# Steps of a triangular inverse offered to two engines, and a TensorE order that stays in a part of the array, in a hybrid gMLP and RWKV-7 block

## The chip, the cores and the metric

One core of a Trainium2 chip runs the whole block in one launch. The metric is the device time of one execution in microseconds (us); the median of three executions is compared. TensorE (PE) multiplies, VectorE (DVE) and ScalarE (ACT) and GpSimd (POOL) work element by element, and the queue of SyncE (SP) issues every DMA.

## The reference

Input and output are 1024 tokens by 1024 channels in float32. What the kernel must compute, cut to what matters here:

```python
def reference(x, ...):
    h = rms_norm(x, norm_pre_g)
    p = h @ w_in                                  # 9344 columns
    ya = gmlp_branch(p[gmlp columns], ...)        # u * (W_s LN(v) + b) * silu(z)
    yb = rwkv7_branch(p[rwkv columns], ...)       # the recurrence below, 16 heads of 64
    merged = sigmoid(ga) * (ya @ w_branch_a) + sigmoid(gb) * (yb @ w_branch_b)
    return x + rms_norm(merged @ w_out, norm_post_g)

def step(state, inp):                             # RWKV-7, for each token of each head
    r_t, w_t, k_t, v_t, kk_t, a_t = inp
    sa = einsum('bhvk,bhk->bhv', state, -kk_t)
    state = state * w_t + outer(sa, kk_t * a_t) + outer(v_t, k_t)
    o_t = einsum('bhvk,bhk->bhv', state, r_t)
```

## The kernel before

The channels lie on the partitions. The large products run as three float32r matmuls of split operands (high by high, high by low, low by high), each 128x128 weights by 512 columns; these are the **dense** matmuls (`ps<-hm,whi`, `ps<-hm,wlo`). The kernel has four stages: the norm and the gMLP branch, up to about 450 us; the RWKV branch, up to about 1240 us, into whose second half the product with `w_branch_a` is laid; the product with `w_branch_b` and the merge; the output product and norm.

The recurrence is computed in chunks of 64 tokens. The function `half_unit` does one **unit**, two heads by 512 tokens (eight chunks); there are 16 units, and every line of it is called once a unit. Its steps, with the names that the profile shows:

1. Preparation: decays, keys and queries are scaled into `W` and `BK`. Two groups of eight matmuls of 64-row weights (`pg<-W,BK`) give the chunk matrices; DVE masks them into `Pm` (the strictly triangular one), `BA` and `W`.
2. The triangular inverse. SP stores the 32x32 diagonal blocks of `Pm` to `bs_d` and loads them back as `X`, so that each of the 128 partitions holds one block; it loads `Q`, the identity. Then the 31 steps of the loop `for t in range(31, 0, -1)`, each a product `qt<-X,Q` and a sum `Q<-Q,qt`, one depending on the other: 62 instructions in a row, with 8 to 76 elements a partition (50 on average). SP stores `Q` to `ts_d` and loads it back as `N`; four DVE transposes write it into `Pm`.
3. Assembling the 64x64 inverse: groups of small matmuls on parts of the array, 32x64 (`pg<-N,Pm`, which is where TensorE first needs the inverse), 64x32, 64x64 and 64x128 (`pg<-BA,X`).
4. The chain over the chunks: `pc<-Z,W`, scaled on ACT and DVE into the next `Z`; then the outputs (`pg<-W,Z`, 128x64), the head norm (`sh`, `sl`, `bdr`), the gate, and a store to `yb_d`, which the third stage loads again.

The order of instructions on every engine is written by `Sched`, a list scheduler. The functions call its queues (`G` for POOL, `V` for DVE, `A` for EITHER); `call` records every instruction, its tiles and an estimated cost, and `flush` lays them out. At each turn it takes, over all engines, the ready instruction that could start first, and among those with an equal start the one of the smallest priority (`CHAIN` 0, `INV` 1, `PREP` 2.5, `LATE` 4, `DENSE` 9). An EITHER instruction is offered to DVE and to POOL; its start on POOL counts as 400 ns (`SLOWER`) later than it is. On TensorE an instruction whose weights need another size of the array than the one before starts `DRAIN` later. The cost rules are linear in the elements: for a two-input instruction `(62 + n) / .96` ns on DVE, and `2.1 * n + 152` on POOL. What the scheduler thinks fixes the order alone; on the chip each engine runs its list from the top and waits where an operand is not there.

Of the kernel before, what the change touches and what calls it, by code (L numbers as in the profile page):

```python
# [14 lines left out]
ALU = mybir.AluOpType  # L15
# [3 lines left out]
P = 128  # L19
# [42 lines left out]
class Sched:  # L62
# [13 lines left out]
            "Sqrt": ("Sqrt",), "Ln": ("Ln",)}  # L76
    SWITCH = 1.5
    SLOWER = 400
    DRAIN = 150

    def __init__(self, nc, tc=None, plan=None):
        self.nc, self.tc, self.plan = nc, tc, plan
# [157 lines left out]
    def flush(self):  # L240
        if self.plan is not None:
            for i in self.plan.orders[self.nflush]:
                self.tc.keep_in_program_order(self.calls[i]())
                self.calls[i] = None
            self.nflush += 1
            return
        ops, b0, n = self.ops, self.done, len(self.ops)
        self.ends += [0.0] * (n - b0)
        self.start += [0.0] * (n - b0)
        ends = self.ends  # L250
        left, succ, users = {}, {}, {}
        for i in range(b0, n):
            d = [j for j in ops[i][1] if j >= b0]
            left[i] = len(d)
            for j in d:
                succ.setdefault(j, []).append(i)
            for t in ops[i][2]:
                users[t] = users.get(t, 0) + 1
        state = self.__dict__.setdefault("state", {})
        where = self.__dict__.setdefault("where", {})  # L260
        lastend = self.__dict__.setdefault("lastend", {})
        self.slot += [None] * (self.ntile - len(self.slot))
        nxt = {}
        for t in range(self.ntile):
            if t not in where:
                nxt.setdefault(self.group[t], []).append(t)
        for g in nxt:
            nxt[g] = nxt[g][::-1]
        ready = {e: [] for e in self.free}

        def push(i):
            for eng in ("DVE", "POOL") if i in self.took else (ops[i][0],):
                t = 0.0
                for j in ops[i][1]:
                    t = max(t, ends[j] + self.LATENCY[ops[j][0]][self.ENGINES.index(eng)])
                ready[eng].append((t, i))

        bank = {}

        def when(t, i, eng):  # L280
            want = {}
            for v in ops[i][2]:
                if v in where:
                    t = max(t, where[v])
                    for e, x in bank.get(v, {}).items():
                        if e != eng:
                            t = max(t, x + 200)
                    continue
                g = self.group[v]
                want[g] = want.get(g, 0) + 1  # L290
                if self.bufs[g][1] and nxt[g][-1] != v:
                    return None
            for g, m in want.items():
                s = state.setdefault(g, [])
                for h in [h for h in self.heirs.get(g, ()) if not nxt.get(h)]:
                    self.heirs[g].remove(h)
                    self.places[g] += [(h, k) for k in range(len(state[h]))]
                    s += state[h]
                m -= max(0, self.bufs[g][0] - len(s))
                if m <= 0:  # L300
                    continue
                f = sorted(lastend[u] for u in s if not users.get(u))
                if len(f) < m:
                    return None
                t = max(t, f[m - 1])
            if ops[i][8]:
                t = max(t, self.port["POOL" if eng == "DVE" else "DVE"])
            return t

        for i in range(b0, n):  # L310
            if left[i] == 0:
                push(i)
        order = []
        while len(order) < n - b0:
            best = None
            for e, r in ready.items():
                for t, i in r:
                    t = when(t, i, e)
                    if t is None:
                        continue  # L320
                    t = max(t, self.free[e])
                    p = ops[i][4]
                    if self.switch(ops[i][5]):
                        p = (p[0] + self.SWITCH, p[1])
                    key = (t + (self.SLOWER if e == "POOL" and i in self.took else 0), p)
                    if best is None or key < best[0]:
                        best = key, e, i, t
            if best is None:
                raise RuntimeError("the schedule is stuck: " + str(
                    [(e, [(i, ops[i][7], [(v, self.group[v]) for v in ops[i][2] if v not in where]) for t, i in r][:6])  # L330
                     for e, r in ready.items()]))
            _, e, i, s = best
            for r in ("DVE", "POOL") if i in self.took else (e,):
                ready[r] = [x for x in ready[r] if x[1] != i]
            eng, deps, tiles, dur, prio, table, size, _, port = ops[i]
            if i in self.took:
                self.took[i] = eng = e
                if e == "POOL":
                    dur = size
                ops[i] = (eng, deps, tiles, dur, *ops[i][4:])  # L340
            for v in tiles:
                if v not in where:
                    g = self.group[v]
                    st = state[g]
                    if len(st) < self.bufs[g][0]:
                        self.slot[v], where[v] = len(st), 0.0
                        st.append(v)
                    else:
                        k = min((k for k in range(len(st)) if not users.get(st[k])), key=lambda k: lastend[st[k]])
                        self.slot[v], where[v] = k, lastend[st[k]]  # L350
                        st[k] = v
                    nxt[g].remove(v)
                    self.used.append(v)
            if eng == "SP":
                self.start[i] = s
                self.free[e] = s + dur
                self.hw = max(s + dur, self.hw) + size[1]
                self.dq = max(self.hw + 650, self.dq) + size[0] / 360.0
                ends[i] = self.dq + 950
            else:  # L360
                if self.switch(table):
                    s += 1290
                if eng == "PE" and size != self.array:
                    self.array, s = size, s + self.DRAIN
                if table:
                    self.table = table if self.table is None or self.switch(table) else self.table
                self.start[i] = s
                self.free[e] = ends[i] = s + dur
                if port:
                    self.port[e] = s + dur  # L370
            order.append(i)
            for v in tiles:
                users[v] -= 1
                if self.group[v][0] == "psum":
                    bank.setdefault(v, {})[eng] = ends[i]
                lastend[v] = max(lastend.get(v, 0.0), ends[i] + (eng != "SP") * 200)
            for k in succ.get(i, ()):
                left[k] -= 1
                if left[k] == 0:
                    push(k)  # L380
        self.orders.append(order)
        self.done = n
# [43 lines left out]
def half_unit(S, I, rw, dram, bank, p, h, r, k0, v, zz, uh, ul, bdr, xw, xa, Z, KI, vec, con, hv, eps, yb):  # L426

    mm, transpose, act, dma = S.PE.matmul, S.PE.transpose, S.ACT.activation, S.SP.dma_start
    V, G, A, at = S.DVE, S.POOL, S.EITHER, S.at
# [89 lines left out]
    for a in range(4):  # L519
        i = a % 2  # L520
        dma(bs_d[:, a].rearrange("c s t -> s c t"), Pm[32 * a:32 * a + 32, :, 32 * i:32 * i + 32])
    B = rw.tile([P, 32, 32], F32, name="X", bufs=2, fifo=False)
    for j in range(4):
        dma(B[32 * j:32 * j + 32].rearrange("p s t -> p (s t)"), bs_d.rearrange("c a s t -> (c a) (s t)"))
    Q = rw.tile([P, 8, 32], F32, name="Q", bufs=2)
    dma(Q.rearrange("p m s -> p (m s)"), I["q0"])
    qt = rw.tile([P, 8, 32], F32, name="qt", bufs=1)
    for t in range(31, 0, -1):
        m0 = t // 4
        G.tensor_tensor(qt[:, m0:, 0:t], B[:, 0:t, t].unsqueeze(1).broadcast_to([P, 8 - m0, t]),  # L530
                        Q[:, m0:, t].unsqueeze(2).broadcast_to([P, 8 - m0, t]), op=ALU.mult)
        G.tensor_tensor(Q[:, m0:, 0:t], Q[:, m0:, 0:t], qt[:, m0:, 0:t], op=ALU.add)
    ts_d = dram.tile([4, 8, 4, 8, 32], F32, name="ts_d", bufs=2)
    dma(ts_d.rearrange("q c a m s -> (q c a) (m s)"), Q.rearrange("p m s -> p (m s)"))
    N = rw.tile([P, 8, 32], F32, name="N", bufs=1)
# [2 lines left out]
    for a in range(4):  # L538
        i = a % 2
# [842 lines left out]
```

## Time and profile before

| | |
|---|---|
| median of 3 executions | 1429.69 us (1426.26 to 1430.96) |
| the profiled execution | 1426.28 us |
| its span, first to last instruction | 1424.1 us |
| busy: PE, DVE, ACT, POOL | 95%, 79%, 52%, 37% |
| mean granted clock of TensorE | 0.976 |
| steps of the inverse | 992 instructions, all on POOL |

A row of the timeline gives the start of an instruction from the span's first, how long it took, engine, line, operation, tiles written and read, shape and count; in square brackets stands the idle time of the engine in front of it and what ended it. All instructions are recorded through one line (L134), so they are told apart by their tiles.

### The profile page before, as it was taken

The page shows a single profiled execution, that of the slowest core. Times are in us where ns is not written, and L with a number is a line of the kernel's source. Part 1 is how long each engine was busy: PE and PEld are TensorE (multiplying, and loading weights), DVE is VectorE, ACT ScalarE, POOL GpSimd, SP SyncE. Part 2 cuts the span into 40 slices and gives each one's busy share as a digit, 9 for nine tenths or more (in the row PEclk, how much of TensorE's full clock was granted, in tenths as well). Part 3 has the DMA queues.
Part 4 walks back from the last instruction along what each step waited for, and adds up shares of the span by engine and source line. Part 5 has one row for each costly group of instructions (what it writes and reads, how often), then busy time and mean ns, then how long its engine had stood idle before and what let it go on. Part 6 is the DMA issues. An engine that isn't in the chain of part 4 may idle for free.

```text
span 1424.1 us, 23358 instructions
## 1 busy us (share of the span) xinstructions
PE 1347.4 (95%) x8390; PEld 1075.0 (75%) x8390; DVE 1118.8 (79%) x2034; ACT 742.6 (52%) x1340; POOL 525.8 (37%) x1135
## 2 busy tenths in 40 slices
PE   5899999999999999999998989999899899979997
PEld 3787888888878777777776767777677677858785
DVE  7977888887865868888788877888788575599957
ACT  6626444444444656667655567666666353433223
POOL 0002000001121176756566663776745553043211
PEclk9899999999999999999999999999999899989999
DMA  7102434447775211222211212211135756254456
GB/s 250 45 1 96 155 134 148 141 140 228 263 249 205 64 56 38 67 71 67 64 46 45 57 53 64 61 54 48 53 99 165 230 177 226 88 202 170 140 215 242
DMA packets 109523, 175.12 MB, mean 123 GB/s; under 512 B 43488, under 2 KB 53856, under 8 KB 109408
## 3 DMA queue, kind: packets, MB, share of 16 engines
q1 hardware_dynamic: 109408, 173.64, 36.8%
q8 instruction: 66, 1.08, 0.3%
q14 instruction: 49, 0.40, 0.1%
HBM read 121.17 MB, written 52.43 MB: 122 GB/s over the span
## 4 chain that ended last, share of the span: by engine, by line
PE 67%; DVE 13%; ACT 9%; DMA 6%; issue 4%; SPq 1%; POOL 1%; DVEq 0%; ACTq 0%; POOLq 0%
PE ps L134 37%; PE pg L134 25%; PE pc L134 5%; DVE hm L134 2%; DVE Pm L134 2%; ACT L134 2%; DVE W L134 1%; DMA hm<-ya_d 1%; DVE pg L134 1%; ACT Z L134 1%; DVE BK L134 1%; DVE wlo L134 1%; SPq L134 1%; ACT BA L134 1%; ACT KI L134 1%
## 5 line engine op out<-in xcount | busy, mean ns | idle before, releaser
L134 PE MATMUL ps<-hm,whi 128*128 128x512 f32 x1616 | 538.7, 405 | 5.3 <-DMA hm<-ya_d 4.7
L134 PEld LDWEIGHTS ps<-hm,whi 128*128 128x128 f32 x1616 | 301.8, 191 | 69.9 <-DMA hm<-ya_d 9.8
L134 PE MATMUL ps<-hm,wlo 128*128 128x512 f32 x808 | 326.8, 405 | 1.1 <-DVE wlo L134 1.1
L134 POOL TENSOR_TENSOR qt<-X,Q 128x60 f32<-128x60 f32 (+24 forms) x496 | 204.5, 412 | 91.3 <-DMA X<-bs_d 39.0
L134 POOL TENSOR_TENSOR Q<-Q,qt 128x60 f32<-128x60 f32 (+24 forms) x496 | 196.1, 395 | 37.9
L134 PEld LDWEIGHTS ps<-hm,wlo 128*128 128x128 f32 x808 | 154.1, 191 | 33.6 <-DVE wlo L134 3.1
L134 PE MATMUL pg<-pg,ring 128*128 128x512 f32 x720 | 168.1, 389 | 0.0
L134 PEld LDWEIGHTS pg<-pg,ring 128*128 128x128 f32 x720 | 135.1, 188 | 28.1
L134 ACT ACT_TABLE_LOAD x75 | 96.2, 1283 | 2.9 <-DVE mv L134 0.9
L134 ACT ACTIVATE whi<-raw 128x1024 fp32r<-128x1024 f32 x64 | 67.4, 1053 | 56.4 <-PE ps L134 30.0
L134 ACT ACTIVATE Z<-pc,gc 64x64 f32<-64x64 f32 x120 | 36.8, 307 | 106.9 <-PE pc L134 104.7
L134 DVE TENSOR_TENSOR wlo<-raw,whi 128x1024 fp32r<-128x1024 f32 x60 | 74.3, 1238 | 10.1 <-ACT whi L134 9.9
L134 POOL TENSOR_TENSOR th<-th 128x512 f32<-128x512 f32 x3 | 4.2, 1406 | 185.2 <-DMA pg<-in_w_o_dram 175.6
L134 ACT ACTIVATE X<-pg 128x512 f32<-128x512 f32 x64 | 36.9, 594 | 43.5 <-PE pg L134 43.0
L134 PE MATMUL ps<-pg,hm 128*128 128x512 f32 x192 | 50.9, 422 | 9.2 <-ACT pg L134 4.4
L134 DVE TENSOR_SCALAR Z<-pc,gc 64x64 f32<-64x64 f32 x120 | 34.8, 290 | 27.1 <-ACT Z L134 19.5
L134 PEld LDWEIGHTS pc<-Z,W 128*128 128x128 f32 x240 | 40.1, 188 | 20.2 <-DVE Z L134 8.3
L134 PEld LDWEIGHTS ps<-pg,hm 128*128 128x128 f32 x192 | 38.3, 202 | 20.2 <-ACT pg L134 5.0
L134 PE MATMUL pc<-Z,W 128*128 128x128 f32 x240 | 50.8, 293 | 1.1 <-ACT Z L134 0.4
L134 POOL TENSOR_TENSOR wlo<-raw,whi 128x1024 fp32r<-128x1024 f32 x4 | 9.9, 2479 | 112.7 <-DVE pg L134 85.0
L134 PE MATMUL pg<-W,BK 64*128 64x128 f32 (+1 forms) x530 | 47.3, 290 | 2.6 <-ACT KI L134 1.6
L134 PEld LDWEIGHTS pg<-W,BK 64*128 64x128 f32 (+1 forms) x530 | 37.7, 187 | 13.9 <-issue 5.4
(793 smaller groups left out, 2738.2 us busy)
## 6 DMA issues: line engine op xcount, KB each, us to landing
raw<-in_w_in_dram SPq DMA_DIRECT2D x65, 512.0 KB, 3.4
X<-bs_d SPq DMA_DIRECT2D x64, 128.0 KB, 2.7
hm<-ya_d SPq DMA_DIRECT2D x32, 256.0 KB, 5.4
wo_d<-sv SPq DMA_DIRECT2D x12, 512.0 KB, 2.7
raw<-in_w_a_dram SPq DMA_DIRECT2D x12, 512.0 KB, 3.3
W<-wo_d SPq DMA_DIRECT2D x10, 512.0 KB, 4.8
sv<-sv_d SPq DMA_DIRECT2D x8, 512.0 KB, 3.3
ya_d<-th SPq DMA_DIRECT2D x8, 512.0 KB, 2.6
```

Of the source, the lines that this page charges most:

```text
L134: self.calls.append(lambda: getattr(e, op)(*a, **k))
```

## The change

```diff
@@ class Sched
     SLOWER = 400
-    DRAIN = 150
+    DRAIN = 195
+    HOLD = 200
@@ flush
                     p = ops[i][4]
+                    late = self.HOLD if e == "PE" and self.array != (P, P) and ops[i][6] != self.array else 0
                     if self.switch(ops[i][5]):
                         p = (p[0] + self.SWITCH, p[1])
-                    key = (t + (self.SLOWER if e == "POOL" and i in self.took else 0), p)
+                    key = (t + late + (self.SLOWER if e == "POOL" and i in self.took else 0), p)
@@ half_unit
     for t in range(31, 0, -1):
         m0 = t // 4
-        G.tensor_tensor(qt[:, m0:, 0:t], B[:, 0:t, t].unsqueeze(1).broadcast_to([P, 8 - m0, t]),
+        A.tensor_tensor(qt[:, m0:, 0:t], B[:, 0:t, t].unsqueeze(1).broadcast_to([P, 8 - m0, t]),
                         Q[:, m0:, t].unsqueeze(2).broadcast_to([P, 8 - m0, t]), op=ALU.mult)
-        G.tensor_tensor(Q[:, m0:, 0:t], Q[:, m0:, 0:t], qt[:, m0:, 0:t], op=ALU.add)
+        A.tensor_tensor(Q[:, m0:, 0:t], Q[:, m0:, 0:t], qt[:, m0:, 0:t], op=ALU.add)
```

The 62 instructions of a unit's inverse are offered to DVE and POOL. While TensorE's last instruction used a part of the array, an instruction that needs another size counts as 200 ns later in the choice (not in the estimated times); a change of size is estimated 45 ns dearer. The work is the same: 6599 matmuls on TensorE in both, and the same instructions elsewhere, except that ScalarE loads its tables 69 times and not 75. In the new order 835 of the 992 steps stand on DVE and 157 on POOL. Nineteen more of the other EITHER instructions stand on POOL. TensorE changes the size of the array 228 times and not 244.

On POOL, in the middle of one unit's inverse (`X` the blocks, `Q` the inverse, `Z` the chain's state), the steps stood in a row:

```order
L134 TENSOR_TENSOR qt_5022<-X_5021,Q_4984 128x4x16
L134 TENSOR_TENSOR Q_4984<-Q_4984,qt_5022 128x4x16
L134 TENSOR_TENSOR qt_5022<-X_5021,Q_4984 128x5x15
L134 TENSOR_TENSOR Q_4984<-Q_4984,qt_5022 128x5x15
L134 TENSOR_TENSOR qt_5022<-X_5021,Q_4984 128x5x14
L134 TENSOR_TENSOR Q_4984<-Q_4984,qt_5022 128x5x14
L134 MEMSET Z_5038 64x64 x2
L134 TENSOR_TENSOR qt_5022<-X_5021,Q_4984 128x5x13
```

On DVE, at the same steps of the same unit in the new order (`W`, `Pm` belong to the next unit):

```order
L135 TENSOR_TENSOR qt_5021<-X_5017,Q_4976 128x4x16
L135 TENSOR_SCALAR Z_5005<-pc_533,gc_4942 64x64
L135 TENSOR_TENSOR Q_4976<-Q_4976,qt_5021 128x4x16
L135 TENSOR_TENSOR Pm_5032<-pg_529,con_61 64x256
L135 TENSOR_TENSOR qt_5021<-X_5017,Q_4976 128x5x15
L135 SCALAR_TENSOR_TENSOR W_5035<-hk_5016,ep_5009 64x4x64
L135 TENSOR_TENSOR Q_4976<-Q_4976,qt_5021 128x5x15
L135 TENSOR_TENSOR W_5035<-r_4998,ep_5009 64x4x64
L135 TENSOR_TENSOR qt_5021<-X_5017,Q_4976 128x5x14
```

Each step now has one other DVE instruction between it and the next. Of the 685 pairs of successive steps that are both on DVE, 510 have something between them and 175 stand next to each other.

On TensorE, in the third unit, a group of eight `pg<-BA,X` (64x128) was broken by a step of the chain, `pc<-Z,W` (128x128):

```order
L134 MATMUL pg_450<-BA_4890,X_4939 128x128
L134 MATMUL pg_449<-BA_4890,X_4939 128x128
L134 MATMUL pc_451<-Z_4896,W_4883 128x128
L134 MATMUL pg_450<-BA_4890,X_4939 128x128
L134 MATMUL ps_452<-hm_1216,whi_1089 128x512
```

In the new order the group of the same unit is whole, and the chain's step follows it:

```order
L135 MATMUL pg_451<-BA_4889,X_4943 128x128
L135 MATMUL pg_452<-BA_4889,X_4943 128x128
L135 MATMUL pc_453<-Z_4895,W_4885 128x128
L135 MATMUL pg_454<-con_61,BK_4957 128x128 x4
L135 MATMUL ps_443<-hm_1225,whi_1086 128x512
```

No group is broken any more.

On SP, behind the last unit's inverse, the four loads of `N` stood behind nine loads of `yb_d`:

```order
L134 DMA ts_d_178<-Q_5349 128x256
L134 DMA ma_d_0_179<-r_5388 128x512
L134 DMA hm_1280<-yb_d_0_163 128x512
L134 DMA hm_1281<-yb_d_0_168 128x512
L134 DMA hm_1282<-yb_d_0_177 128x512
L134 DMA hm_1283<-yb_d_0_138 128x512
L134 DMA hm_1284<-yb_d_0_143 128x512
L134 DMA hm_1285<-yb_d_0_148 128x512
L134 DMA hm_1286<-yb_d_0_153 128x512
L134 DMA hm_1287<-yb_d_0_157 128x512
L134 DMA hm_1288<-yb_d_0_163 128x512
L134 DMA N_5402<-ts_d_178 32x8x32 x4
```

In the new order one load stands between:

```order
L135 DMA ts_d_176<-Q_5337 128x256
L135 DMA r_5397<-ga_d_0_104 128x512
L135 DMA N_5398<-ts_d_176 32x8x32 x4
L135 DMA ma_d_0_177<-r_5386 128x512
L135 DMA raw_1175<-in_w_a_dram 128x1024
```

## Rows read from the trace of the kernel before

**Rows 1.** The page: span, and busy time, share and instructions of each engine.

```profile
span 1424.1 us, 23358 instructions
PE 1347.4 (95%) x8390; PEld 1075.0 (75%) x8390; DVE 1118.8 (79%) x2034; ACT 742.6 (52%) x1340; POOL 525.8 (37%) x1135
```

**Rows 2.** Waits of PE: who waited for whom, us in total, times, longest.

```profile
PE pg L134 <- DVE Pm L134: 13.0, 8, 3.3
...
PE pg L134 <- DVE hm L134: 4.5, 1, 4.5
```

**Rows 3.** Timeline, all engines, from an inverse's last step to its use.

```profile
744.10 0.22 POOL L134 TENSOR_TENSOR Q<-Q,qt 128x8 f32<-128x8 f32 x1
...
745.54 0.42 SPq L134 DMA_DIRECT2D ts_d<-Q  x1
...
748.01 2.57 SPq L134 DMA_DIRECT2D N<-ts_d  x4
...
752.24 1.84 DVE L134 STREAM_TRANSPOSE Pm<-N 32x256 f32<-32x256 f32 x4 [0.98 <-DMA N<-ts_d]
...
752.73 0.42 PE L134 MATMUL pg<-N,Pm 32*64 32x32 f32 x2 [3.32 <-DVE Pm L134]
```

**Rows 4.** Timeline, PE: two of the other three such waits.

```profile
839.88 0.27 PE L134 MATMUL pg<-N,Pm 32*64 32x32 f32 x2 [2.53 <-DVE Pm L134]
...
1205.33 0.27 PE L134 MATMUL pg<-N,Pm 32*64 32x32 f32 x2 [2.55 <-DVE Pm L134]
```

**Rows 5.** Windows: stretch, busy us (instructions) of PE, PEld, DVE, ACT, POOL; PEclk, DMA, GB/s.

```profile
752.80:759.50 6.70, 6.18 (x70) 4.91 (x71) 5.00 (x10) 1.38 (x3) 5.53 (x16) 0.50 0.05 19
```

**Rows 6.** Windows: twelve units, from the first unit's assembling to the thirteenth's.

```profile
539.00:1057.00 518.00, 497.17 (x4047) 388.94 (x4045) 424.48 (x848) 334.68 (x596) 324.29 (x796) 0.98 0.20 57
```

**Rows 7.** The page: a group of instructions with busy us, mean ns, idle before.

```profile
L134 POOL TENSOR_TENSOR qt<-X,Q 128x60 f32<-128x60 f32 (+24 forms) x496 | 204.5, 412 | 91.3 <-DMA X<-bs_d 39.0
```

**Rows 8.** Timeline, POOL: the first step of the inverse that ends in rows 3.

```profile
708.58 0.25 POOL L134 TENSOR_TENSOR qt<-X,Q 128x31 f32<-128x31 f32 x1
```

**Rows 9.** Timeline, DVE: a tiny instruction, a pair without and a pair with a dependence.

```profile
606.80 0.16 DVE L134 TENSOR_TENSOR k<-k,edge 128x1 f32<-128x1 f32 x1 [1.38 <-ACT k L134]
...
609.67 0.42 DVE L134 SCALAR_TENSOR_TENSOR W<-hk,ep 64x256 f32<-64x256 f32 x1
610.01 0.42 DVE L134 TENSOR_TENSOR W<-r,ep 64x256 f32<-64x256 f32 x1
...
749.00 0.75 DVE L134 SCALAR_TENSOR_TENSOR oc<-oc,vec,osq 128x512 f32<-128x512 f32 x1 [0.45 <-ACT osq L134]
749.79 0.75 DVE L134 SCALAR_TENSOR_TENSOR oc<-oc,vec,bon 128x512 f32<-128x512 f32 x1
750.57 0.69 DVE L134 TENSOR_TENSOR oc<-oc,zz 128x512 f32<-128x512 f32 x1
```

**Rows 10.** Timeline, PE: dense matmuls before and behind a group on half the array.

```profile
629.67 0.40 PE L134 MATMUL pg<-sh,bdr 128*128 128x512 f32 x1
629.90 0.39 PE L134 MATMUL ps<-hm,whi 128*128 128x512 f32 x1
630.22 1.16 PE L134 MATMUL pg<-BA,X 64*128 64x128 f32 x16
631.31 0.50 PE L134 MATMUL pg<-sl,bdr 128*128 128x512 f32 x1
631.65 0.39 PE L134 MATMUL ps<-hm,whi 128*128 128x512 f32 x1
```

**Rows 11.** Timeline, SP: the store and the loads of the last inverse.

```profile
1187.88 0.42 SPq L134 DMA_DIRECT2D ts_d<-Q  x1
...
1196.27 2.62 SPq L134 DMA_DIRECT2D N<-ts_d  x4
```

**Rows 12.** Third stage: windows as in rows 5, and a row of PE's timeline.

```profile
1271.60:1281.80 10.20, 5.29 (x11) 3.50 (x12) 10.02 (x16) 0.00 (x0) 2.89 (x2) 0.50 0.63 207
...
1278.10 1.22 PE L134 MATMUL ps<-wlo,raw 128*128 128x512 f32 x2 [3.29 <-DVE wlo L134]
```

## The prediction

> **What bounds the kernel now.** I read the page first. TensorE is busy 95% of a span of 1424.1 us, VectorE 79%, GpSimd 37% [rows 1]. A view of the whole can't say more: TensorE has the same 6599 matmuls before and after, so the time can only change by what TensorE waits, by its clock, and by what it pays for changes of the array's size. So the second view is that of TensorE's own waits. One line leads it: waits on `Pm`, the inverse that DVE transposes into place, 13.0 us in 8 pieces [rows 2]. The timeline shows what they are. The last step on GpSimd begins at 744.10; SP stores Q at 745.54 and begins the loads of N at 748.01; the transposes run at 752.24; TensorE, idle for 3.32 us, starts at 752.73 [rows 3]. The reader is to see that everything behind the last step is fixed in length (8.4 us here), so what is late is the inverse itself. Three more waits look like this [rows 4], each in two pieces, which makes the eight.
>
> The third view is the clock. In the 6.7 us from 752.80, right behind the wait, the granted clock is 0.50, TensorE's lower level, after 0.98 on the mean of the stage [rows 5, 6]; a stretch of the same length stands behind each of the other three waits. At half clock 6.8 us hold 3.4 us of work.
>
> Why is the inverse late? The step on GpSimd is estimated at 2.1 ns an element and 152 ns, for 50 elements 0.26 us. The trace has 0.41 us [rows 7], and the chain of 62 that ends in rows 3 ran from 708.58 to 744.32, 35.7 us, or 0.58 us a step with the gaps between [rows 3, 8]. The order of TensorE was written for a faster inverse than the chip has.
>
> **What the change removes.** The four waits, 13.0 us. The four stretches of half clock cost 4 x 3.4 = 13.7 us, but about 0.6 us in each was already counted, as the second piece of its wait; I take 11.5. A wait goes only if what replaces it is not late too; that is the next part but one.
>
> **The array's size.** Between dense matmuls the starts lie 0.23 us apart (629.67, 629.90). Into a group on half the array it is 0.32 (to 630.22), and the first dense one behind it holds its successor back 0.34 (631.31 to 631.65) [rows 10]. The last small one of the group to the first dense adds about as much again, since the group's 16 in 1.09 us are 0.07 apart on the mean and nothing can overlap at its end: between 0 and 0.2. So a way in and out costs 0.2 to 0.4, I take 0.36. The order has 16 changes fewer, 8 ways in and out: 2.9 us. The bounds are 1.6 and 3.2.
>
> **What VectorE takes on.** 835 steps, 52 a unit. No row of before has this step on DVE; the nearest are two-input instructions of 1 element, 0.16 us, and of 512, 0.69 us [rows 9]. A line between them gives 0.21 us for 50 elements. How much of it holds DVE up depends on the neighbour: two instructions that don't depend on each other start 0.34 apart though each takes 0.42, so the next starts 0.08 early; a dependent one starts 0.04 after the end (749.00, 0.75 long, then 749.79) [rows 9]. A step costs 0.13 or 0.25; with 175 of 685 pairs side by side, 0.16 on the mean, 8.4 us a unit.
>
> The twelve units of rows 6 took 518 us, 43.2 each. DVE was busy 424.5, 35.4 a unit, and idle 7.8. So 35.4 + 8.4 = 43.8 at the most. At the least, each of the 71 instructions a unit (848 over 12) gives back the 0.08 us that its busy time counts in front of a wait which a step now fills: 38.1. I take 39, near the lower end, since most steps stand between two other instructions and since the nineteen instructions that moved to GpSimd take about a microsecond a unit off. Without the three waits of this stretch and their clock ((13.0 + 11.5) x 3/4 = 18 us) TensorE needs (518 - 18) / 12 = 41.7 a unit. So DVE fits, with 2.7 us a unit to spare, a share of 93%. This is the step of the sum that I trust least.
>
> At this place a rule of the Trainium skill speaks against the change. The page "VectorE: DVE Perf Modes", section "The TRN2 errata", says that SBUF-sourced instructions pay a fixed extra each, so that many small ones pay it over and over, and section "The DRAIN you can't avoid" that the next doesn't start until the pipe is empty. By that a step would hold DVE for its whole 0.21 us, 11 us a unit. The trace agrees with the fixed part (0.16 us for one element) but not with the second: the starts of 609.67 and 610.01 overlap [rows 9]. By that rule DVE would need 35.4 + 11 = 46.4 us a unit.
>
> **Is the new inverse in time?** Between a unit's first and last step stand, in the new order, 23 to 35 us of DVE's work at these prices, 30.5 on the mean, its own steps included. The 157 steps on GpSimd are covered: beside each one stands at least 0.5 us of other DVE work, against the 0.41 of rows 7. So the inverse takes about 31 to 34 us; the one in rows 3 and 8 took 35.7. It is hardly shorter. What changes is that the order of TensorE now knows it. I counted TensorE's matmuls between a unit's last `pg<-W,BK` and its first `pg<-N,Pm` at the starts of rows 10: 48.4 us on the mean before, 45.8 now. That the mean is 2.6 lower is no danger by itself, as it goes with the shorter inverse; but the eighth and ninth units have 41.8 and 37.6, and an inverse of 31.6 and 28.4. There TensorE will wait: 4.0 + 8.2 below the mean, 12 us in all with clock. Bounds: 0, and 16 x 2.6 = 42 us if no inverse is shorter than before.
>
> **The end of the stage.** Behind the last inverse SP held the loads of N back from 1187.88 to 1196.27, 8.4 us against 2.5 in rows 3 [rows 3, 11]; now one load stands between and not nine. The last unit's `pg<-N,Pm` stands 13 us of TensorE's work earlier, with more of the product with `w_branch_a` behind it. So `yb` is ready some 13 us earlier for the third stage, whose start waits for sums on DVE: 4.5 us [rows 2], 3.3 at 1278.10, and 10.2 us at a clock of 0.50 around them, in which TensorE was busy 5.3 [rows 12]. All of it together is 11 us. But DVE was busy 10.0 of these 10.2 us, so its own queue is part of the cause. I take half, 6; bounds 0 and 11.
>
> **The sum.** 13.0 + 11.5 + 2.9 + 6 - 12 = 21.4 us less: a span of 1402.7. The profiled execution took 1426.28 with a span of 1424.1, so 1404.9. The median of the three runs shown is 3.4 above the profiled one; against it I forecast 1408 us, 1.5% less. The six table loads of ScalarE cost nothing: it is not busy enough to matter.
>
> **The rivals.**
>
> *VectorE sets the pace.* It runs its list in order, so the waits that it keeps add to the 39. It decides from 43.2 - 39 = 4.2 us of waits a unit; before, it had 7.8. For it speaks that a step which waits for GpSimd or for a load of X now holds up the masks and evictions that TensorE waits for, in the same queue. Against it: the steps were put where DVE waited. If 6 us stay, a unit takes 45: 1.8 x 13 = 23 us more, less 2.9 for the array, with no gain at the end: a span of 1444, as a median 1450. Chance 20%.
>
> *Each small instruction holds VectorE for its whole 0.21 us*: 52 x 0.21 = 11 us and 35.4 make 46.4 a unit, 3.2 x 13 = 42 us more than 43.2, less 2.9: a span of 1463, as a median 1469. Against it speak the overlapping starts [rows 9]. Chance 5%. This is the rule of the Trainium skill's page "VectorE: DVE Perf Modes", section "The DRAIN you can't avoid".
>
> *The order is as wrong as before.* The inverse is nearly as long as it was, the room for it 2.6 us shorter; the 24.5 us of waits and clock stay at other units, and what the end and the array give (8.9) goes into longer waits, four of 2.6. Then 1426 to 1430, no change. For it: the inverse of 31 to 34 us. Against it: DVE's estimate, (62 + n) / .96, is 0.12 us for 50 elements, close to the 0.13 from the rows, where GpSimd's was 0.26 for 0.41. Chance 15%.
>
> **How the numbers follow.** Forecast 60% (alone 1394 to 1420, from the bounds 0 and 11 of the end and up to 24 of new waits). What a measurement of this kernel can tell from no change is 0.3%, 4 us. Faster: the forecast's 60 and a quarter of the last rival's 15, less a little for its upper edge, 62%. Same: 12%. Slower: the first two rivals and the rest, 26%. The range reaches to about the first rival's time: 1388 to 1448.
>
> **What would show it.** Right: no wait of TensorE on `Pm` over 2 us but for one or two about the eighth and ninth units; a clock of 1.00 from 540 to 1050 but there; DVE at 90 to 95% in that stretch, with the step at 0.21 us; twelve units in 500 to 506 us; less idle time at the start of the third stage. Wrong: steps longer than 0.25 us, or DVE at 98% and TensorE waiting for masks (`W`, `Pm`, `BK`) or weights (`wlo`): the first rivals. Waits on `Pm` as many as before: the last.

## The result, and the profile after

The changed kernel takes 1472.76 us (median of 4 runs, 1470.1 to 1475.17), against 1429.61 for the kernel before: a ratio of 1.0305 [1.028, 1.033]. It is 3% slower, where 1.5% faster was forecast, and outside the range. The profiled span grew by 49.3 us, from 1424.1 to 1473.4.

The page after, which answers to [rows 1], and the groups of the inverse's steps, which answer to [rows 7] (busy us, mean ns | idle before them and what ended it):

```profile
span 1473.4 us, 23482 instructions
PE 1361.5 (92%) x8390; PEld 1074.8 (73%) x8390; DVE 1247.9 (85%) x2850; ACT 738.3 (50%) x1334; POOL 210.3 (14%) x319
...
DVE 43%; PE 36%; DMA 7%; issue 6%; ACT 4%; SPq 2%; POOL 0%; DVEq 0%; ACTq 0%; POOLq 0%
...
L135 DVE TENSOR_TENSOR qt<-X,Q 128x54 f32<-128x54 f32 (+23 forms) x418 | 104.0, 249 | 11.8 <-DMA X<-bs_d 5.4
L135 DVE TENSOR_TENSOR Q<-Q,qt 128x60 f32<-128x60 f32 (+21 forms) x417 | 95.2, 228 | 7.1 <-POOL qt L135 0.5
L135 POOL TENSOR_TENSOR Q<-Q,qt 128x66 f32<-128x66 f32 (+18 forms) x79 | 27.0, 342 | 246.6 <-DVE qt L135 225.6
```

Its line in the middle gives the chain of work that ended last, as shares of the span by engine. In the page before it was:

```profile
PE 67%; DVE 13%; ACT 9%; DMA 6%; issue 4%; SPq 1%; POOL 1%; DVEq 0%; ACTq 0%; POOLq 0%
```

The reader is to see three things. That chain now runs over VectorE for 43%, where it was 13%. A step takes 0.239 us there on the mean, not 0.21. And GpSimd, left with 157 steps, spends its time in waits for VectorE.

The waits of TensorE (us in total, times, longest), which answer to [rows 2]:

```profile
PE pc L135 <- DVE Z L135: 19.0, 42, 1.9
PE pg L135 <- DVE W L135: 14.9, 17, 1.7
...
PE pg L135 <- DVE Pm L135: 5.5, 11, 1.9
PE pg L135 <- DVE N L135: 4.7, 8, 1.6
```

The long waits on `Pm` are gone, as forecast. In their place stand many short ones, on `Z`, the state that goes from chunk to chunk, and on the masked `W`: things that VectorE computes in the same list as the steps. The twelve units of [rows 6], now from 533.3 to 1108.1 (columns as there):

```profile
533.30:1108.10 574.80, 518.33 (x4067) 395.16 (x4066) 522.27 (x1466) 328.65 (x590) 85.27 (x186) 0.97 0.18 53
```

A unit takes 574.8 / 12 = 47.9 us, against 43.15 (from the first use of `N` at 539.4 to the thirteenth's at 1057.2). VectorE is busy for 43.5 of them, 91%. The first unit starts 6.1 us earlier than before, twelve units take 57.0 more, and all that follows 1.6 less: that is the 49.3.

### The profile page after: what moved, and what is told of

Read it like the earlier page. It is cut to its first block, busy times and chain, and to the rows that moved or that the text cites. A ratio compares the mean times of both kernels' runs of the same rounds, so it can differ in the third digit from the quotient of the medians.

```text
span 1473.4 us, 23482 instructions
## 1 busy us (share of the span) xinstructions
PE 1361.5 (92%) x8390; PEld 1074.8 (73%) x8390; DVE 1247.9 (85%) x2850; ACT 738.3 (50%) x1334; POOL 210.3 (14%) x319
## 4 chain that ended last, share of the span: by engine, by line
DVE 43%; PE 36%; DMA 7%; issue 6%; ACT 4%; SPq 2%; POOL 0%; DVEq 0%; ACTq 0%; POOLq 0%
PE ps L135 20%; PE pg L135 14%; DVE W L135 7%; DVE qt L135 5%; DVE Q L135 4%; DVE Pm L135 3%; PE pc L135 3%; DVE BK L135 2%; DVE wlo L135 2%; DVE Z L135 2%; SPq L135 2%; DVE hm L135 2%; DVE k L135 2%; DMA X<-bs_d 1%; DVE zz L135 1%
## 5 line engine op out<-in xcount | busy, mean ns | idle before, releaser
L135 PEld LDWEIGHTS ps<-hm,wlo 128*128 128x128 f32 x808 | 153.5, 190 | 33.8 <-DVE wlo L135 4.3
L135 DVE TENSOR_TENSOR qt<-X,Q 128x54 f32<-128x54 f32 (+23 forms) x418 | 104.0, 249 | 11.8 <-DMA X<-bs_d 5.4
L135 DVE TENSOR_TENSOR Q<-Q,qt 128x60 f32<-128x60 f32 (+21 forms) x417 | 95.2, 228 | 7.1 <-POOL qt L135 0.5
L135 ACT ACTIVATE Z<-pc,gc 64x64 f32<-64x64 f32 x120 | 36.9, 307 | 124.9 <-PE pc L135 115.2
L135 PEld LDWEIGHTS pc<-Z,W 128*128 128x128 f32 x240 | 37.1, 189 | 62.1 <-DVE Z L135 48.2
L135 PE MATMUL pc<-Z,W 128*128 128x128 f32 x240 | 56.5, 318 | 25.1 <-DVE Z L135 19.0
L135 POOL TENSOR_TENSOR Q<-Q,qt 128x66 f32<-128x66 f32 (+18 forms) x79 | 27.0, 342 | 246.6 <-DVE qt L135 225.6
L135 ACT ACTIVATE X<-pg 128x512 f32<-128x512 f32 x64 | 36.7, 592 | 46.7 <-PE pg L135 46.5
L135 POOL TENSOR_TENSOR qt<-X,Q 128x60 f32<-128x60 f32 (+18 forms) x78 | 27.7, 355 | 216.1 <-DVE Q L135 207.6
L135 DVE TENSOR_TENSOR W<-pg,con 64x512 f32<-64x512 f32 x64 | 44.0, 688 | 1.4
```

Source lines behind the costliest of these rows:

```text
L135: self.calls.append(lambda: getattr(e, op)(*a, **k))
```

## A measure for VectorE's list

For the comparisons below I work out one number from each trace: what VectorE's list *needs* in a unit, which is the period less the idle pieces over 0.15 us (its waits), over the same twelve units. The short gaps between neighbours stay in it, since nothing can fill them. Need and waits add up to the period by this definition; what the table can show is which of the two moves. The orders mix a unit with other work in different ways, so a difference under 1 us a unit means little.

| kernel | steps on VectorE a unit | need | waits | period | median us |
|---|---|---|---|---|---|
| before | 0 | 36.3 | 6.9 | 43.15 | 1429.6 |
| e1 order only | 0 | 36.4 | 5.8 | 42.2 | 1406.8 |
| e11 HOLD alone | 0 | 36.4 | 6.5 | 43.0 | 1404.4 |
| e10 order, relief | 0 | 32.6 | 9.3 | 41.9 | 1395.6 |
| e15 no inverse | 0 | 34.5 | 7.2 | 41.6 | 1396.5 |
| e12 few steps | 7.4 | 37.5 | 4.0 | 41.4 | 1402.0 |
| e13 relief, few steps | 7.3 | 33.8 | 7.8 | 41.6 | 1407.5 |
| e8 free split | 26.6 | 40.2 | 5.7 | 45.9 | 1463.0 |
| e6 half of each | 26.6 | 42.6 | 2.4 | 45.0 | 1431.0 |
| e9 changed, relief | 56.5 | 42.7 | 2.6 | 45.2 | 1443.6 |
| changed kernel | 51.8 | 45.2 | 2.7 | 47.9 | 1472.8 |
| e3 true prices | 52.3 | 45.2 | 2.3 | 47.4 | 1464.6 |
| e2 steps only | 51.8 | 45.5 | 2.8 | 48.2 | 1488.1 |
| e14 load, no inverse | 51.8 idle ones | 45.2 | 1.0 | 46.2 | 1481.4 |
| e7 all on VectorE | 62.8 | 48.2 | 1.6 | 49.7 | 1506.0 |
| e5 idle load | 52 idle ones | 51.1 | 3.7 | 54.8 | 1600.2 |
| e4 before, price | 0 | 36.9 | 10.5 | 47.4 | 1475.5 |

Up to a need of some 38 us the period stays at 41.4 to 43.2, TensorE's own: in e1, for one, TensorE is busy for 97% of it, against 90% in the changed kernel. From 42 on there are 1 to 4 us of waits left and the period goes with the need. e8 and e4, which fit neither, have more waits; they are spoken of below.

## Experiments

Theory A: VectorE's list has become longer than TensorE's work in a unit, and sets the pace. The rivals came up one by one: B, the new preference on TensorE is what hurts; C, the load fits, but the order was built with too short steps; D, of the kernel before, the inverse is too long whatever the order knows; E, the hand-overs of a chain that changes queues cost the time; F, each new order is a draw of luck. "The order-only kernel" is e1. Ratios are to the kernel before.

**e1, only HOLD and DRAIN.** The diff without its last part: the steps stay with `G`.

> Only HOLD and DRAIN; all 992 steps stay on GpSimd. Theory A (VectorE's list has become longer than TensorE's work of a unit): as before, 1420 to 1432 us, VectorE's busy time in twelve units 35 to 36 us a unit, the period 43 us. Rival B (the new preference on TensorE makes the order worse, the steps are harmless): 1460 to 1480 us, as the changed kernel.

Measured: 1406.79 us, 0.9855 [0.983, 0.988]. B has fallen, and more: this half of the change is worth 1.5%, below what A expected too. TensorE's waits on `Pm`:

```profile
PE pg L135 <- DVE Pm L135: 5.2, 8, 2.2
```

**e2, only the steps.**

```
-    DRAIN = 195
-    HOLD = 200
+    DRAIN = 150
-                    late = self.HOLD if e == "PE" and ...
```

> Only the steps go to EITHER; no HOLD, DRAIN as before. Theory A: 1465 to 1480 us, as the changed kernel, with a unit every 47 to 48.5 us and VectorE over 90% busy. Rival B: 1425 to 1435 us, as before.

Measured: 1488.09 us, 1.0432 [1.041, 1.045], a unit every 48.2 us. As A had it, a little over its range. e1 and e2 split the change: the order gives 1.5%, the steps take 4.3%; together they make about the 3%.

**e3, true prices in the plan.**

```
-            return (62 + n) / .96 + 63 * ptr, None, 0
+            small = op == "tensor_tensor" and n < 256
+            return ((151 if small else 62) + n) / .96 + 63 * ptr, None, 0
...
-            return 2.1 * n + 152, None, 0
+            return 2.1 * n + (152 if n > 256 else 300), None, 0
```

> The changed kernel, but the list scheduler is told what a step takes: on VectorE (151 + n) / .96 in place of (62 + n) / .96 for a two-input instruction of under 256 elements, 0.21 us for 50, and on GpSimd 300 + 2.1 n in place of 152 + 2.1 n, 0.41 us. The split hardly moves: 819 steps stay on VectorE in place of 835, so it is the order alone that knows better. Theory A: the load is the same, so 1450 to 1475 us. Rival C (the load fits, only the order built with too short steps is wrong): 1405 to 1435 us, with no wait of TensorE on Z and W over 2 us.

Measured: 1464.63 us, 1.0271 [1.025, 1.030]. C has fallen: a planner that knows the step's length gains 8 us of the 43. The steps (825 in the end) stay on VectorE; the 400 ns against GpSimd decide that, as e8 shows, which leaves them out.

**e4, the kernel before with the true price on GpSimd.** The last line of e3's diff alone.

> The kernel before, all steps on GpSimd, but a step is estimated at 300 + 2.1 n ns there in place of 152 + 2.1 n (0.41 us for 50 elements, as the trace has it). It tests the first step of the prediction, that TensorE waited 13 us on Pm because its order was written for a faster inverse. If so: the waits on Pm and their half clock go, 1398 to 1412 us. Rival D (the inverse is too long for what TensorE has to do beside it, whatever the order knows): 1424 to 1440 us, with the same idle time elsewhere.

Measured: 1475.5 us, 1.0343 [1.030, 1.038]: far over both, so it decides neither for the prediction's step nor for D. No step is on VectorE here, so this is a third way to be slow. GpSimd's waits in twelve units, of this kernel and then of the one before:

```profile
POOL ep L134 <- DVE W L134: 66.4, 7, 12.7
POOL Z L134 <- PE pg L134: 55.3, 5, 11.4
POOL gc L134 <- ACT ep L134: 38.5, 12, 6.2
```

```profile
POOL ep L134 <- DVE W L134: 34.9, 9, 9.6
...
POOL gc L134 <- ACT ep L134: 28.6, 9, 9.4
...
POOL Z L134 <- PE pg L134: 12.9, 6, 3.1
```

In the new list the small fills of `ep` and `Z` and the copy `gc` stand between the steps and wait for other units' work, 14.5 us of each inverse against 4.0 (the mean of the first thirteen units); it takes 44.7 us from its first step to its last, against 34.3. So an estimate nearer the truth can still make a worse list, and orders alone can cost 3%: F had to be tried.

**e5, an idle load.**

```
+        d = qd[:, 0:(8 - m0) * t].rearrange("p (m s) -> p m s", m=8 - m0)
+        V.tensor_tensor(d, B[:, 0:t, t]..., B[:, m0:8, t]..., op=ALU.mult)
+        if t > 10:
+            V.tensor_tensor(d, d, d, op=ALU.add)
```

> The order-only kernel (1407 us), all 992 steps of the inverse on GpSimd, and 832 instructions on VectorE that nobody needs: 52 a unit, of the steps' forms, that read X and write a scratch tile of their own; they wait for the load of X alone and nobody waits for them. Theory A (VectorE's list is too long, whatever the added instructions compute): VectorE needs 34 us for its other work, 11 for these and some 2 of waits, 47 a unit, so 1440 to 1475 us. Rival E (what costs is the hand-over from step to step on a queue with other work, and between VectorE and GpSimd): 1403 to 1420 us.

Measured: 1600.16 us, 1.1216 [1.119, 1.125]. Over both, so E has not passed, and A's size is off by 125 us. The load was not what I meant it to be. Beside GpSimd's steps one of these takes 0.29 us on the mean; they come in bunches (between 540 and 1060 us one follows directly on another 319 times, against 84 in the changed kernel); and the clock falls to 0.88:

```profile
537.10:1194.70 657.60, 534.79 (x4060) 418.20 (x4060) 586.06 (x1470) 331.49 (x590) 302.48 (x813) 0.88 0.16 46
```

**e6, half of each inverse.**

```
-        G.tensor_tensor(qt[...
+        (A if t < 16 else G).tensor_tensor(qt[...
```
(the same for `Q`)

> The order-only kernel, with the second half of each inverse (t under 16, 30 steps of 62) given to EITHER; the first half stays on GpSimd. 427 steps land on VectorE, 27 a unit. Theory A as a threshold (VectorE needs 34 + 27 x 0.21 + 2.4 = 42.1 us a unit, TensorE 42.2): 1400 to 1418 us. As a price that each step has wherever it stands, (1472.8 - 1406.8) / 835 = 0.079 us: 1441 us, 1432 to 1450.

Measured: 1431.01 us, 1.0042 [1.002, 1.006]: 13 us over the range of the threshold, and a microsecond under that of a price for each step, so that by itself it speaks for the price; e12 decides between the two. The need rose by 6.2 us for 26.6 steps, 0.23 each and not 0.21 or less, so that with its waits it is 45.0, already over TensorE's 42. The threshold lies lower than I had put it.

**e7, all steps on VectorE** (`V` in place of `G`).

> The order-only kernel with all 992 steps on VectorE, none on GpSimd, so that no step waits for the other engine. Theory A: 34 + 62 x 0.21 + 2 = 49 us a unit, 1480 to 1510 us. Rival E (hand-overs between the two engines, of which the changed kernel had 65 each way in the twelve units' waits, are the price): under 1455 us.

Measured: 1506.04 us, 1.0561 [1.053, 1.059], a unit every 49.7 us. As A had it. No step waits for the other engine here, and it is the slowest of the splits: the price needs no hand-over between engines.

**e8, a free split** (`SLOWER = 0`).

> The changed kernel without the 400 ns by which the list scheduler holds a step back from GpSimd (SLOWER 0). 439 steps land on VectorE, about as many as where the second half of each inverse was given to it, but scattered along the chain of 62, so with many hand-overs. Theory A (the load alone counts): within 10 us of that kernel, 1400 to 1420 us. Rival E (hand-overs count): over 1435 us, or 20 us or more above it.

Measured: 1462.99 us, 1.0259 [1.024, 1.028], 32 us over e6 with as many steps on VectorE, as E had it. VectorE's waits in the twelve units:

```profile
DVE Q L135 <- POOL qt L135: 19.8, 51, 0.6
DVE W L135 <- PE pg L135: 11.1, 10, 2.0
DVE qt L135 <- POOL Q L135: 10.4, 28, 0.5
```

Waits for GpSimd add 30.2 us, 2.5 a unit, to a list that runs in order, so hand-overs do cost. But of the 31.5 us of span only 10.7 lie in these units; 27.2 lie behind them, 6.4 are won in front, and the 27.2 I did not take apart. In the twelve units of the changed kernel VectorE waits for GpSimd (over 0.15 us) a single time:

```profile
DVE Q L135 <- POOL qt L135: 0.5, 1, 0.5
```

So waits of this kind are not its price. Whether the load alone is, was left to e14.

**e9 and e10, relief of VectorE**, in the changed and in the order-only kernel.

```
-        V.tensor_scalar(Zn[O, cn, 1, :], pS[O, 1], gc[O, c, :], None, op0=ALU.mult)
+        act(Zn[O, cn, 1, :], pS[O, 1], AF.Copy, scale=gc[O, c, :])
...
-        V.tensor_copy(Pm[a:a + 32, :, 32:64], p2[a:a + 32])
+        act(Pm[a:a + 32, :, 32:64], p2[a:a + 32], AF.Copy)
...
-    V.tensor_scalar(Y, py, con[:, C_LOW:C_LOW + 1], None, op0=ALU.mult)
+    act(Y, py, AF.Copy, scale=con[:, C_LOW:C_LOW + 1])
```

> The changed kernel with some of VectorE's other work given to ScalarE: the odd head's half of Z (90 instructions in twelve units, 26.1 us there), the copies into Pm (24, 9.9 us) and the scaling of Y (12, 5.7 us): 3.5 us a unit. 884 steps stay on VectorE, 49 more than in the changed kernel, which takes about 0.5 us a unit back. Theory A (the period of a unit is what VectorE's list takes, 45.2 us and 2.7 of waits): the period falls from 47.9 by the same 3.0 us, 39 us in all: 1434 us, 1420 to 1446. Rival F (the list scheduler's orders differ by chance, and the changed kernel's is an unlucky one): no relation to the load, 1455 to 1490 us, with VectorE idle for the time that it was given.

> The same relief of VectorE by 3.5 us a unit in the order-only kernel (1407 us), where all steps are on GpSimd. Theory A: VectorE needs 36.4 us of a unit of 42.2 there and sets nothing, so relief brings nothing: 1400 to 1415 us. If relief is worth the same 39 us here, 1368 us, then it isn't the steps' load that it takes away.

Measured: e9 1443.62 us, 1.0118 [1.008, 1.016]; e10 1395.6 us, 0.9787 [0.977, 0.981]. The windows of the twelve units, of e9 and of e10:

```profile
534.60:1077.10 542.50, 509.65 (x4086) 394.40 (x4085) 494.77 (x1406) 383.08 (x728) 70.72 (x148) 0.99 0.21 57
```

```profile
538.00:1041.00 503.00, 488.20 (x4059) 382.39 (x4058) 383.12 (x724) 379.33 (x724) 323.99 (x791) 1.00 0.21 59
```

In e9 the need falls by 2.5 us and the period by 2.7; VectorE stays at 91%. The relief gives 29 us where VectorE is the bound, all of it in the twelve units. e9 also takes a `Z` on which TensorE waited out of VectorE's list, so it can't tell the load from `Z`'s place in the list; e14 can. In e10 the need falls by 3.8 us and the period by 0.3, so there VectorE only idles longer. Its 1395.6 us lie below the 1400 to 1415 expected all the same: of the 13.2 us of span that it gains on e1, 10.1 are won behind the twelve units (351.1 us against 361.2), which I did not take apart. F has fallen for the changed kernel, whose time goes with the load. e10 beats both kernels.

**e11, HOLD alone** (DRAIN 150).

> The kernel before with HOLD 200 alone, DRAIN as before (150). It tells which of the two numbers made the order-only kernel 1.5% faster. If it is the preference for work on the part of the array in use (HOLD): 1400 to 1412 us. If it is the dearer change of the array in the plan (DRAIN), or both: 1415 to 1432 us.

Measured: 1404.41 us, 0.9847 [0.983, 0.986]. The preference for work on the part of the array in use is what gains; the dearer change of the array adds nothing to it (by itself it was not run). TensorE's waits on `Pm`:

```profile
PE pg L135 <- DVE Pm L135: 2.2, 7, 0.4
```

**e12, few steps** (`A if t < 5 else G`).

> The order-only kernel with the last four columns of each inverse (t under 5, 8 steps of 62) given to EITHER: 120 steps land on VectorE, 7.5 a unit. Theory A as a threshold: VectorE needs 36.4 + 7.5 x 0.2 = 38 us, under TensorE's 42, so nothing is lost, and the end of the inverse, which TensorE waits for, comes some 2 us earlier: 1396 to 1412 us. A price of 0.079 us for every step: 1416 us. Rival F (any new order is a draw): anything from 1400 to 1475 us.

Measured: 1402.04 us, 0.9828 [0.981, 0.985], a unit every 41.4 us. In A's range, and 14 us below what a price for each step gives: below the threshold steps on VectorE cost nothing.

**e13, e10's relief and e12's few steps together.**

> The two edits that gained, together: VectorE relieved by 3.5 us a unit of work that ScalarE can do, and the last 8 steps of each inverse given to EITHER (117 on VectorE), in the order-only kernel. VectorE needs 34 us of a unit of 41.5, so by theory A nothing that it does sets the pace, and both gains may stand: 1383 to 1398 us, at or below the relief alone (1396). If the two took the same waits away: 1394 to 1404 us.

Measured: 1407.52 us, 0.9873 [0.985, 0.990], over both. The unit is as short as in either (41.6 us), but what follows the twelfth takes 362.9 us, against 351.1 in e10. Below the threshold orders differ by some 10 us for reasons that I didn't follow.

**e14 and e15, no inverse, with and without an idle load.**

```
-        G.tensor_tensor(qt[...   and   G.tensor_tensor(Q[...
+        V.tensor_tensor(qt[:, m0:, 0:t], B[:, 0:t, t]..., B[:, m0:8, t]..., op=ALU.mult)
+        if t > 10:
+            V.tensor_tensor(qt[:, m0:, 0:t], qt[:, m0:, 0:t], qt[:, m0:, 0:t], op=ALU.add)
```

> The order-only kernel with the 992 steps left out (Q stays as it was loaded, so the inverses are missing), and 832 instructions of their forms on VectorE, 52 a unit, that read X and write qt and for which nobody waits. GpSimd has nothing of the inverse to do, so none of them meets it. Theory A (the load alone): VectorE needs 36.4 + 52 x 0.17 to 0.25, 45 to 49 us, and 2 to 3 of waits: a unit every 47.5 to 52 us, 1465 to 1530 us, with instructions of 0.24 us on the mean in place of the 0.29 of the idle load beside GpSimd's steps. Rival E (the hand-overs of the chain make the time): within 15 us of the kernel without the inverse and without the load.

> The same without the 832 instructions: the 992 steps are left out and nothing stands for them. It is the floor, what a faster inverse could have been worth at the most: 1375 to 1405 us, VectorE at 36.4 us a unit as in the order-only kernel.

Measured: e14 1481.44 us, 1.0386 [1.036, 1.041]; e15 1396.49 us, 0.9785 [0.977, 0.980]. The 832 instructions of e14, whose results nobody reads, cost 85 us:

```profile
L135 DVE TENSOR_TENSOR qt<-X 128x60 f32<-128x60 f32 (+24 forms) x496 | 125.4, 253 | 14.2 <-DMA X<-bs_d 6.5
L135 DVE TENSOR_TENSOR qt<-qt 128x31 f32<-128x31 f32 (+6 forms) x336 | 73.1, 218 | 5.5
```

Their mean is 0.239 us and the need 45.2, both as in the changed kernel. The load alone is enough, with 1.0 us of waits a unit where the changed kernel has 2.7. With e7, and with the one wait for GpSimd in the changed kernel, that settles A against E. e15 shows the other side: with no inverse at all the order-only kernel would be 10 us faster, no more than the orders below the threshold differ by anyway, so a faster inverse had little to offer.

## Why the prediction was wrong

*The step that failed is "What VectorE takes on".* It bounded VectorE's demand at 38.1 to 43.8 us a unit and took 39. The need is 45.2, 8.9 over the 36.3 of before. It splits into 11.1 for the steps and 34.1 for the rest of the list, where the prediction had 8.4 and 39 - 8.4 = 30.6. So two terms were too small. A step was priced at 0.16 us; from its start to the next one's it holds VectorE for 0.214 (133.0 us for 622 in the twelve units, without the waits behind them). It takes 0.239 and not 0.21, and only 313 of the 622 are followed by a start before their end, where 510 of 685 were counted on. And the other instructions were to give back the last 0.08 us of their time in front of waits that the steps would fill, 35.4 - 30.6 = 4.8 a unit in the 39; the rest of the list shrank by 36.3 - 34.1 = 2.2. The trace of before could have told: it has 9 waits over 0.15 us a unit, so 9 x 0.08 = 0.7 us was there to give back in this way, and the 35.4 leaves out 0.9 us of short gaps. The rows of the timeline, VectorE, which answer to [rows 9]:

```profile
690.71 0.21 DVE L135 TENSOR_TENSOR Q<-Q,qt 128x60 f32<-128x60 f32 x1
690.84 0.68 DVE L135 SCALAR_TENSOR_TENSOR ta<-ta,hk 128x512 f32<-128x512 f32 x1
691.44 0.29 DVE L135 TENSOR_TENSOR qt<-X,Q 128x76 f32<-128x76 f32 x1
...
699.05 0.26 DVE L135 TENSOR_TENSOR qt<-X,Q 128x65 f32<-128x65 f32 x1
699.34 0.29 DVE L135 TENSOR_SCALAR Z<-pc,gc 64x64 f32<-64x64 f32 x1
699.66 0.23 DVE L135 TENSOR_TENSOR Q<-Q,qt 128x65 f32<-128x65 f32 x1
```

Neighbours on all 128 partitions overlap (690.71 to 690.84, 691.44 before 691.52). `Z`, on partitions 64 to 127, starts 0.03 behind the end of the one in front, and the one behind it does too. I read the one pair of [rows 9] that overlaps as the rule. In the twelve units 520 of 589 pairs on 128 partitions, in which the second reads nothing of the first's, start early (0.08 us on the mean), but of 761 pairs with one on 64 or 32 partitions 492 start behind (0.03). The kernel before has 334 such pairs in its twelve units too, and they are in its 36.3. The 158 more cost 158 x 0.11 / 12 = 1.4 us a unit against early starts, an estimate; so this is a part of the 6.2 us that were missing and not the whole.

The rule of the Trainium skill that was set against the change ("The DRAIN you can't avoid") came close in its result: its 46.4 us a unit is nearer to 45.2 than my 39, and its 11 us for the steps is what they take. In part that is luck, since half of the steps are followed by an early start. Why a start is held in one pair and not in the next, the same page of the Trainium skill, "VectorE: DVE Perf Modes", says in another section, "Two Vector instructions with no wait between them", in what it calls a model: an instruction starts only when all earlier ones on VectorE have finished if an input or its output starts in another group of 32 partitions than the last that was read from, or written to, the same memory. The trace agrees: in the twelve units a step follows directly on a `Z` 83 times, and each time starts 0.03 us behind its end. It was read from the trace and not tried by itself.

*The first rival came true*, at nearly the second's price. VectorE kept 2.7 us of waits, less than the 4.2 from which it was to decide, but on 45.2 and not 39; the sum of 47.9 is over the 43.2 named. I had given these two 25%. The signs named would not have told it: VectorE at 91% and a step under 0.25 us stood on the side of "right"; the waits on `W` and the length of the twelve units stood on the other.

*"What the change removes"* was right in what happens and wrong in what does it. The waits on `Pm` fell from 13.0 to 5.5 us, but to 5.2 in e1 and 2.2 in e11, where no step has moved. The preference on TensorE, which I priced at 2.9 us by changes of the array alone, made the gain of 18.9 us of span (1424.1 to 1405.2); that it agrees with my forecast in size is an accident of the sum. Nor did the waits give back what they were counted at. The prediction placed 18 us of waits on `Pm` and half clock in the twelve units. In e11 the waits on `Pm` are nearly gone, but the twelve units take 515.5 us against 517.8, with 25 more matmuls in them (some 6 us at the 0.23 of [rows 10], an estimate), and the granted clock is 0.98 as before: half clock now stands behind other waits.

```profile
539.39:1054.89 515.50, 498.99 (x4071) 391.06 (x4070) 425.77 (x854) 335.08 (x599) 326.66 (x808) 0.98 0.21 58
...
664.17 0.50 PE L135 MATMUL pg<-sh,bdr 128*128 128x512 f32 x1 [2.15 <-ACT sh L135]
...
665.70:672.50 6.80, 6.80 (x72) 4.98 (x74) 3.77 (x8) 2.74 (x4) 4.66 (x15) 0.50 0.14 48
```

Of the 21.9 us of span that e11 gains, 19.6 lie behind the twelve units, and why stays open.

*"The order was written for a faster inverse than the chip has"* is not shown: with the true price (e4) the waits on `Pm` fell to 4.8 us and the list paid 3% elsewhere, but with the old price they fell to 2.2 us in e11. That everything behind the last step is fixed in length was a reading of one unit: in the kernel before the last of the four transposes starts 8.3 to 10.9 us behind it in the first thirteen units, and 14.1 to 22.7 in the last three.

*The inverse* was to take 31 to 34 us. Over the first thirteen units its mean is 36.7, against 34.3 before, as its steps stand in a full list.

*The new waits at the eighth and ninth unit* were one, shorter than the 12 us given to them, with half clock behind it:

```profile
873.79 0.30 PE L135 MATMUL pg<-N,Pm 32*64 32x32 f32 x2 [1.90 <-DVE Pm L135]
...
873.79:880.60 6.81, 5.97 (x70) 4.70 (x70) 6.60 (x21) 0.81 (x1) 0.34 (x1) 0.53 0.12 42
```

*The end of the stage* was to give 6 us. All that follows the twelve units is 1.6 us shorter, with the last units in it: from the thirteenth's first use of `N` to the sixteenth's it is 8.4 us less, and from there to the end 6.8 more. The new order moves work across that border, so how much the end gave stays open.

*The range of the forecast alone* doesn't follow from the bounds named for it: an end of 0 to 11 and new waits of 0 to 24 around 6 and 12 make 1391 to 1426, not 1394 to 1420. The result lies outside either.

## What to carry to other kernels

Before work goes to an engine that is 80% busy, work out what its list needs in the stage that counts, with the gaps between neighbours, and take the upper end: only e12's dose, 7 steps a unit, which kept the need below TensorE's unit, came free. When a change has two halves, price each half by itself; here the one that I had priced at 2.9 us made the gain, and the one that I had built the gain on took three times as much away. A change of a preference or an estimate in a list scheduler is a change of every queue: here from 1.5% faster (e1, e11) to 3.4% slower (e4).

## Not expected of the hardware

- A two-input step of 50 elements on the mean takes 0.22 us on VectorE with nothing on GpSimd at the time (788 steps of the changed kernel), and 0.30 beside a step of GpSimd (715 of the idle instructions of e5; 99 of them with nothing beside took 0.21). Of the steps of the changed kernel 15 start inside a large two-input instruction of GpSimd, and each ends 0.03 to 0.08 us behind that instruction's end; in the twelve units this adds some 0.9 us a unit. One of them holds up `Z` and TensorE behind it (changed kernel, all engines):

```profile
705.62 1.90 POOL L135 TENSOR_TENSOR sl<-sq,sh 128x512 fp32r<-128x512 f32 x1 [0.88 <-ACT sh L135]
...
706.32 1.28 DVE L135 TENSOR_TENSOR qt<-X,Q 128x49 f32<-128x49 f32 x1
...
708.41 0.29 DVE L135 TENSOR_SCALAR Z<-pc,gc 64x64 f32<-64x64 f32 x1
...
708.75 0.49 PE L135 MATMUL pc<-Z,W 128*128 128x128 f32 x2 [1.92 <-DVE Z L135]
```

- A VectorE that is 91% busy was full here: the other 4.4 us of a unit are short gaps between neighbours (1.7) and waits (2.7).
